# Halving the last two products of a down projection, and of a pair of value pieces, in front of runs of 256-column matmuls

## The chip, the cores and the metric

The kernel runs on one core of a Trainium2 chip. The metric is the device time of one execution in microseconds, as the median of several runs. Profiles are of one execution; a profile's span goes from its first to its last instruction, which is a little less than the time of the execution.

## The reference

A decoder trunk of two layers on 256 tokens of width 1024, in float32. The first layer mixes tokens by dilated sliding-window attention, the second by forgetting attention; each is followed by a SwiGLU feed-forward part.

```python
D_MODEL = 1024; SEQ = 256; DEPTH = 2; N_HEADS = 16; HEAD_DIM = 64
D_FF = 2816

def swiglu(h, w_gu, w_down):
    gu = h @ w_gu
    g, u = gu[..., :D_FF], gu[..., D_FF:]
    return (jax.nn.silu(g) * u) @ w_down

def reference(x, ...):
    h = x
    for i in range(DEPTH):
        j = i // N_MIXERS
        if i % N_MIXERS == 0:
            h = h + dilated_mixer(rmsnorm(h, a_norm[j]), a_w_in[j], a_w_out[j])
        else:
            h = h + forgetting_mixer(rmsnorm(h, b_norm[j]), b_w_in[j], b_f[j], b_w_out[j])
        h = h + swiglu(rmsnorm(h, ffn_norm[i]), ffn_w_gu[i], ffn_w_down[i])
    return rmsnorm(h, final_norm)
```

The dilated mixer projects to queries, keys and values of three groups (window and dilation 128/1, 512/4, 2048/16), the forgetting mixer to one set of queries, keys and values and a gate; both end in an output projection `w_out`.

## The kernel before

**Products in three parts.** Every large matrix product is taken in float32r, with each operand split into a high and a low part: ScalarE writes the high part (line 73), VectorE the rest (line 74). `mm3` then issues three matmuls into the same PSUM tile: high by high (line 172), high by low (173), low by high (174). Its `stat` operand is the stationary one, of 128 columns, for which TensorE loads weights before each matmul; `mov` is the moving one, of 256 or 512 columns. Each matmul instruction has a weight load of its own, also where two in a row use the same stationary block.

**Weights.** `weights` hands out the weights piece by piece (128 x 2048) in the order of the list `order`, and starts the loads of two pieces ahead. `piece` loads a piece in two halves over SyncE's queue, each of which is then split by ScalarE and VectorE. `wh` and `wl` have four buffers, `raw` five.

**Projections.** `proj_feat` computes 128 output features for all 256 tokens: stationary are the weights, moving is `xt` (the normed input, features on partitions), so these are runs of 256-column products, 8 x 3 = 24 for each call, 48 for a piece with two calls. `proj_tok` has 128 tokens stationary and 256 weight columns moving. `proj_pair` computes two value pieces together, with the 512 columns of a half piece moving; it is called once for each half of the contraction (`half` 0, then 1), for both halves of the tokens (`t`), four `k` each, so 24 products of 512 columns.

**First layer.** The list `a_units` sets the order: for each of four quads of heads the queries and keys of three groups (`proj_feat`), and value pieces by `proj_pair` or `proj_tok`. Score, transpose and value matmuls of a quad (`scores_a`, `trans_a`, `pv_a`) are put behind later units by `later`. The scores of group 0 also go through `mm3`, 12 products of 256 columns for each pair of heads (tiles `kr` and `qz` in the profile).

**Feed-forward part (`ffn`).** There are 22 pieces of gate and up weights (`gu`) and 11 of down weights (`dn`). `up_with` computes the gate and up columns of a piece by two calls of `proj_feat` (tiles `ps_mm` and `ps_tr`), and the gated product from them (lines 671, 673). `down(j, t)` adds the part of down weights `j` to the accumulators of token half `t`: two blocks of 512 output columns (tiles `ps_sc` for `t` 0 and `ps_o` for `t` 1), two halves `f` of the contraction each, so 4 x 3 = 12 products. The loop is

```python
for f in range(2, NF):
    if f > 2:
        up(f)
    if f % 2 == 0:
        j = f // 2 - 1
        dn[j] = weights(f"dn{l}", j)
        down(j, 0)
        if j < LATE:
            down(j, 1)
```

with `NF` 22 and `LATE` 8. In the steady part two `up` (96 products of 256 columns) alternate with two `down` (24 of 512). From `j` = 8 on, the second token half's `down` is put off to the end. The last `up` (piece 21) has a higher priority, by which the scheduler puts it ahead of `down(9, 0)`, so that three `up` (144 products) follow `down(8, 0)`. In the last `down` of the second layer (`own`) the upper 512 columns go in two blocks of 256.

The order on each engine is that of the program, apart from such priorities, and is fixed before the run; engines wait for one another by semaphores.

Of the kernel before, what the change touches and what calls it, by code (L numbers as in the profile page):

```python
# [19 lines left out]
KT = D // P  # L20
# [11 lines left out]
def trunk(ctx: ExitStack, tc: tile.TileContext, T, out):  # L32
    nc = tc.nc
# [6 lines left out]
    ALL = slice(None)  # L40

    def first():

        return tc.high_priority(offset=300)

    def psum(tag):
        return ps.tile([P, 512], F32, tag=tag, name=f"ps_{tag}", bufs=2)
# [65 lines left out]
    NJ = NF // 2  # L113
    LATE = NJ - 3
# [13 lines left out]
    def weights(nm, i):  # L128
        upto = order.index((nm, i)) + AHEAD
        while state["next"] <= min(upto, len(order) - 1):  # L130
            key = order[state["next"]]
            ready[key] = piece(key)
            state["next"] += 1
        return ready.pop((nm, i))
# [32 lines left out]
            split(xt, lambda x: x[:, half * 4:half * 4 + 4, t * P:(t + 1) * P],  # L167
                  tr.rearrange("p (k c) -> p k c", k=4))

    def mm3(o, stat, mov, start, stop):  # L170
        (sh, sl), (mh, ml) = stat, mov
        nc.tensor.matmul(o, sh, mh, start=start, stop=False)  # L172
        nc.tensor.matmul(o, sh, ml, start=False, stop=False)  # L173
        return nc.tensor.matmul(o, sl, mh, start=False, stop=stop)  # L174

    def both(pair, *idx):
        return tuple(x[idx] for x in pair)


    def early(x, b):  # L180

        x = x.rearrange("p (n b) -> p b n", b=2)
        return x if b is None else x[:, b]
# [17 lines left out]
    def proj_pair(xt, w, os, half, ts=range(2), by_time=False):  # L201

        for t in ts:
            for k in range(half * 4, half * 4 + 4):
                i = k % 4 * 512
                st = both(xt, ALL, k, ALL)
                last = mm3(os[t], [early(x, t) if by_time else x[:, t * P:(t + 1) * P] for x in st],
                           both(w, ALL, slice(i, i + 512)), k == 0, k == KT - 1)
        return last

    def proj_feat(xt, w, o, c, hook=None):

        last = None
        for k in range(KT):
            between(k, hook, last)
            last = mm3(o, both(w, ALL, slice(k * 256 + c * P, k * 256 + (c + 1) * P)),
                       both(xt, ALL, k, ALL), k == 0, k == KT - 1)
        return last


    def p_tile(n=512, dtype=F32, name="p"):
        return ap.tile([P, 768], dtype, tag="p", name=name, bufs=6)[:, :n]
# [60 lines left out]
    o = psum("o")  # L283
# [10 lines left out]
    for i, c in enumerate(room):  # L294
        b = 1 + (i > 1)
        n = S + 512
# [35 lines left out]
    def square(i):  # L332
        return nc.scalar.activation(part[i].rearrange("p (j s) -> p j s", s=S), xs[i], AF.Square, scale=D ** -0.5)
# [5 lines left out]
    for k in range(KT):  # L339
        if k % 4 == 0:  # L340
            w = tuple(wp.tile([P, 2048], F32R, tag=y, name=y, bufs=4) for y in ("wh", "wl"))
        g, u = g_a[:, k:k + 1], slice(k % 4 * 512, k % 4 * 512 + 512)
        with first(), in_order(cut):
            if k == 0:
                a = nc.vector.tensor_scalar(hi[:, k], xk[k], g, None, op0=ALU.mult)
            else:
                a = nc.scalar.activation(hi[:, k], xk[k], AF.Copy, scale=g)
            b = nc.vector.scalar_tensor_tensor(lo[:, k], xk[k], g, hi[:, k].bitcast(F32), op0=ALU.mult,
                                               op1=ALU.subtract)
            with in_order((a, b)):  # L350
                cut = split(w, lambda y: y[:, u], wk[k])
        if k in (1, 5, 7):
            with first(), in_order(cut):
                a = [square(i) for i in {1: (0, 1), 5: (2,), 7: (3,)}[k]][-1]
                cut = (a, plus(part[0], part[1]) if k == 1 else cut[1])
        for y, z in ((0, 0), (1, 0), (0, 1)):
            for t in range(2):
                nc.tensor.matmul(lead[t], xt[y][:, k, t * P:(t + 1) * P], w[z][:, u], start=k + y + z == 0,
                                 stop=k == KT - 1 and z == 1)
# [7 lines left out]
    with first(), in_order(cut):  # L367
        a = square(4)
# [124 lines left out]
    for i, (hq, g, w) in enumerate(a_units):  # L493
        quad = quads[hq]
        if i == 3:
            o = o_next
        elif i:
            wt = weights("a_in", hq * 9 + g * 3 + w)
        if i != 3 and (w < 2 or g == 0 and hq > 1):
            o = psum("mm")  # L500
# [7 lines left out]
        if i in (24, 31):  # L508
            x.append(hrow("x"))
            t = len(x) - 1  # L510
            nc.sync.dma_start(x[t], T["x"][t * P:(t + 1) * P, :])
        if w < 2:
# [35 lines left out]
            elif g == 0:  # L548

                y = ap.tile([P, 2, 2, S], F32R, tag="h", name="kr", bufs=4)  # L550
                f, q = q, (y[:, 0], y[:, 1])
                split(q, lambda y: y.rearrange("p a (b n) -> p a b n", b=2), f.rearrange("p a (n b) -> p a b n", b=2))
            quad["fm"][g, w] = q
            if w == 1:

                j = i + (hq == 0)
# [5 lines left out]
                if g == 2:  # L562
                    later(j + 1, softmax_a, quad)
                    j = 9 * hq + 11 + 2 * (hq == 0)
# [80 lines left out]
    def ffn(l, hs, xt, grow, mid):  # L645
        acc = {}
        acts = {}

        def act(f):
            if f % 2 == 0:  # L650
                acts[f // 2] = tuple(p_tile(512, F32R, f"a{y}") for y in "hl")
            return acts[f // 2], lambda y: y[:, (f % 2) * S:(f % 2 + 1) * S]

        def gated(g, u, shape):
            sa = ap.tile([P, 512], F32, tag="qr", name="sa", bufs=3)
            sg, a = (sa[:, i * S:(i + 1) * S].rearrange("p (a b) -> p a b", a=shape) for i in range(2))
            nc.scalar.activation(sg, g, AF.Silu)
            nc.vector.tensor_tensor(a, u, sg, op=ALU.mult)
            return a

        def up(f):
            wt = weights(f"gu{l}", f)
            with first() if f == NF - 1 else nullcontext():
                up_with(f, wt)

        def up_with(f, wt):
            sa = ap.tile([P, 512], F32, tag="qr", name="sa", bufs=3)
            sg, a = (sa[:, i * S:(i + 1) * S] for i in range(2))
            g, u = (psum(tag)[:, :S] for tag in ("mm", "tr"))
            proj_feat(xt, wt, g, 0)  # L670
            nc.scalar.activation(sg, g, AF.Silu)  # L671
            proj_feat(xt, wt, u, 1)
            nc.vector.tensor_tensor(a, u, sg, op=ALU.mult)  # L673
            split(*act(f), a)

        def down(j, t, by_f=None):

            wt = dn[j]
            if j == 0:
                acc[t] = [psum(("sc", "o")[t]) for _ in range(2)]  # L680
            cols = [(0, 512, acc[t][0][:, :512]), (512, 512, acc[t][1][:, :512])]
            own = l == 1 and t == 1 and j == NJ - 1
            if own:

                acc[t][1:] = psum("mm"), psum("tr")
                cols[1:] = (512, 256, acc[t][1][:, :256]), (768, 256, acc[t][2][:, :256])
            nf = [(c, f) for c in cols for f in range(2)]
            if by_f is not None:
                nf = [(c, f) for f in by_f for c in cols]
            for (a, b, o), f in nf:  # L690
                i = mm3(o, both(acts[j], ALL, slice(f * S + t * P, f * S + (t + 1) * P)),
                        both(wt, ALL, slice(f * D + a, f * D + a + b)), f == 0 and (j == 0 or own and a >= 512),
                        f == 1 and (j == NJ - 1 or l * t * a > 0 and j == NJ - 2))
            return i


        dn = {}
        head = []
        for f in range(3):
            head.append((weights(f"gu{l}", f), psum((("o", "o", "mm"), ("mm", "mm", "o"))[l][f])))  # L700
            proj_tok(xt, head[f][0], head[f][1][:, :S], 0,
                     hook=(2, lambda: norm_t(*hs[1], grow, xt, 1)) if f == 2 else None)
        for f in range(3):
            o = head[f][1]
            proj_tok(xt, head[f][0], o[:, S:], 1)
            ov = o.rearrange("p (a c b) -> p a c b", a=2, c=2)
            a = gated(ov[:, :, 0, :], ov[:, :, 1, :], 2)
            tr = psum("tr")
            for t in range(2):
                nc.tensor.transpose(tr[:, t * P:(t + 1) * P], a[:, t, :], ident)  # L710
            split(*act(f), tr[:, :S])
# [3 lines that stand above are left out]
            if f % 2 == 0:  # L715
                j = f // 2 - 1
                dn[j] = weights(f"dn{l}", j)
                down(j, 0)
                if j < LATE:
                    down(j, 1)  # L720
        dn[NJ - 1] = weights(f"dn{l}", NJ - 1)
        down(LATE, 1)
        last = down(NJ - 1, 0, (0, 1))
        res = [residual(acc[0], hs[0][0], f"hf{l}0")]
        with tc.issue_after(last.ins):
            down(NJ - 2, 1)
            if l == 0:
                down(NJ - 1, 1, (0,))
            else:
                h1 = hs[1][0][:, 512:]  # L730
                with first():
                    nc.vector.tensor_tensor(h1, acc[1][1], h1, op=ALU.add)
            mid(res[0])
            down(NJ - 1, 1, (1,) if l == 0 else None)
        res.append(residual(acc[1], hs[1][0], f"hf{l}1") if l == 0 else (acc[1], hs[1][0]))
        return res
# [9 lines left out]
    def mid(h0):  # L746
        nxt["g"] = load_grow(2)
        nxt["xt"] = xt_tile()
        norm_t(*h0, nxt["g"], nxt["xt"], 0)

    hs = ffn(0, hs, xt, g_f, mid)
    xt, g_b = nxt["xt"], nxt["g"]

# [121 lines left out]
    for i in range(2):  # L875
        last = proj_pair(xt, ws[i], os, i, (1,))
# [6 lines left out]
    for i, (hq, w) in enumerate(b_units):  # L883
# [3 lines left out]
        o = psum("mm")  # L887
        if w < 2:
# [15 lines left out]
            if w == 1:  # L904
                j = i + 1
# [35 lines left out]
    for o, (a, b) in zip(acc, ((0, 512), (512, 256), (768, 256))):  # L941
        s = slice(a, a + b)
# [108 lines left out]
```

## Time and profile before

| | |
|---|---|
| median of 3 runs | 771.75 us (771.35 to 771.86) |
| the profiled execution | 771.89 us |
| its span | 770.0 us |
| TensorE busy | 759.2 us (99%), 5760 matmuls |
| weight loads busy | 703.2 us (91%), 5760 |
| VectorE, ScalarE busy | 509.9 us (66%), 401.0 us (52%) |
| DMA | 135.01 MB, 175 GB/s in the mean |
| TensorE clock granted | 0.999 |

In the timeline a row gives the start and the length of an instruction in microseconds, its engine, its line, and the tiles it writes and reads (output, then sources). Matmuls overlap: the next one starts before the record of the last one ends, so the distance between two starts tells what a matmul costs, and its recorded length does not. A row ending in x1 is a single instruction. In a row of the view by stretches stand the stretch, its length, and for TensorE, weight loads, VectorE, ScalarE and GpSimd the busy time and the number of instructions, then the clock, the share of the DMA engines and GB/s. A row of waits says which engine waited for which, the total, how often and the longest.

### The profile page before, as it was taken

What the parts mean: (1) busy time and instruction counts of PE and PEld (TensorE: products, weight loads), DVE (VectorE), ACT (ScalarE), POOL (GpSimd) and SP (SyncE); (2) the same over time, 40 slices, a digit from 0 to 9 for tenths busy, and PEclk for the clock granted to TensorE, in tenths of its full rate; (3) what the DMA queues carried; (4) which work ended last, traced back from release to release, by engine and by line L of the source; (5) the groups of instructions that cost most, each with busy time, mean ns of one, the idle gap of its engine ahead of it and who ended that gap; (6) DMA issues with size and microseconds to landing.
All of it is one profiled execution on the core that took longest, in us unless ns stands there. A gap on an engine that the chain in (4) does not pass through costs nothing.

```text
span 770.0 us, 14046 instructions
## 1 busy us (share of the span) xinstructions
PE 759.2 (99%) x5760; PEld 703.2 (91%) x5760; DVE 509.9 (66%) x758; ACT 401.0 (52%) x664; POOL 33.8 (4%) x51
## 2 busy tenths in 40 slices
PE   9999999999999999999999999999999999999996
PEld 7998999999998799999999988999889999999995
DVE  6998987976978476545456374887756645456533
ACT  7745639448538455434454354586655444344421
POOL 1110000010010000000000003100000000000000
PEclk9999999999999999999999999999999999999999
DMA  8865461743663267565566444644326665656601
GB/s 319 288 206 170 162 217 57 242 168 98 202 213 120 95 222 240 181 194 189 186 202 231 147 156 145 218 139 128 115 92 220 216 206 175 198 186 206 204 2 54
DMA packets 38352, 135.01 MB, mean 175 GB/s; under 512 B 4368, under 2 KB 5648, under 8 KB 38288
## 3 DMA queue, kind: packets, MB, share of 16 engines
q1 hardware_dynamic: 38144, 134.01, 52.4%
q8 instruction: 45, 0.74, 0.4%
q14 instruction: 19, 0.16, 0.1%
q10 hardware_dynamic: 144, 0.10, 0.0%
HBM read 133.05 MB, written 1.05 MB: 174 GB/s over the span
## 4 chain that ended last, share of the span: by engine, by line
PE 86%; DVE 5%; ACT 3%; issue 2%; DMA 2%; POOL 1%; SPq 0%; POOLq 0%; DVEq 0%; ACTq 0%
PE ps_mm L172 15%; PE ps_mm L174 15%; PE ps_mm L173 15%; PE ps_tr L172 5%; PE ps_tr L174 5%; PE ps_tr L173 5%; PE ps_sc L174 4%; PE ps_sc L172 4%; PE ps_sc L173 4%; PE ps_o L174 3%; PE ps_o L173 3%; PE ps_o L172 3%; PE ps_tr L265 2%; PE ps_o L276 2%; DVE wl L74 2%
## 5 line engine op out<-in xcount | busy, mean ns | idle before, releaser
L73 ACT ACTIVATE wh<-raw 128x1024 fp32r<-128x1024 f32 x236 | 243.2, 1055 | 224.4 <-PE ps_tr L173 70.5
L74 DVE TENSOR_TENSOR wl<-raw,wh 128x1024 fp32r<-128x1024 f32 x236 | 284.2, 1220 | 104.7 <-ACT wh L73 104.5
L172 PE MATMUL ps_mm<-xt,wh 128*128 128x256 f32 x816 | 229.2, 281 | 0.0
L174 PE MATMUL ps_mm<-xt,wl 128*128 128x256 f32 x816 | 227.7, 279 | 0.1
L173 PE MATMUL ps_mm<-xt,wh 128*128 128x256 f32 x816 | 227.5, 279 | 0.0
L174 PEld LDWEIGHTS ps_mm<-xt,wl 128*128 128x128 f32 x816 | 154.8, 190 | 0.5 <-DVE wl L74 0.5
L173 PEld LDWEIGHTS ps_mm<-xt,wh 128*128 128x128 f32 x816 | 153.5, 188 | 0.9
L172 PEld LDWEIGHTS ps_mm<-xt,wh 128*128 128x128 f32 x816 | 153.2, 188 | 1.1
L173 PE MATMUL ps_tr<-xt,wh 128*128 128x256 f32 x304 | 85.3, 281 | 0.0
L174 PE MATMUL ps_tr<-xt,wl 128*128 128x256 f32 x304 | 85.3, 281 | 0.0
L172 PE MATMUL ps_tr<-xt,wh 128*128 128x256 f32 x304 | 85.1, 281 | 0.0
L673 DVE TENSOR_TENSOR sa<-ps_tr,sa 128x256 f32<-128x256 f32 x38 | 16.1, 425 | 81.6 <-PE ps_tr L174 81.4
L172 PE MATMUL ps_mm<-wh,xt 128*128 128x256 f32 (+1 forms) x176 | 59.6, 339 | 1.6 <-DVE fm L402 1.6
L173 PE MATMUL ps_mm<-wl,xt 128*128 128x256 f32 (+1 forms) x176 | 58.5, 332 | 0.0
L174 PE MATMUL ps_mm<-wh,xt 128*128 128x256 f32 (+1 forms) x176 | 58.4, 332 | 0.0
L174 PEld LDWEIGHTS ps_tr<-xt,wl 128*128 128x128 f32 x304 | 58.3, 192 | 0.0
L173 PEld LDWEIGHTS ps_tr<-xt,wh 128*128 128x128 f32 x304 | 57.1, 188 | 0.0
L172 PEld LDWEIGHTS ps_tr<-xt,wh 128*128 128x128 f32 x304 | 56.9, 188 | 0.0
L172 PEld LDWEIGHTS ps_mm<-wh,xt 128*128 128x128 f32 x176 | 33.5, 190 | 5.5 <-issue 2.0
L174 PEld LDWEIGHTS ps_mm<-wh,xt 128*128 128x128 f32 x176 | 33.5, 190 | 3.6 <-DVE xt L74 0.3
L173 PEld LDWEIGHTS ps_mm<-wl,xt 128*128 128x128 f32 x176 | 33.5, 190 | 2.9
L671 ACT ACTIVATE sa<-ps_mm 128x256 f32<-128x256 f32 x38 | 14.3, 381 | 33.5 <-PE ps_mm L174 33.5
(237 smaller groups left out, 1154.2 us busy)
## 6 DMA issues: line engine op xcount, KB each, us to landing
raw<-in_gu SPq DMA_DIRECT2D x88, 512.0 KB, 4.7
raw<-in_a_in SPq DMA_DIRECT2D x68, 512.0 KB, 4.5
raw<-in_dn SPq DMA_DIRECT2D x44, 512.0 KB, 4.7
raw<-in_b_in SPq DMA_DIRECT2D x24, 512.0 KB, 5.0
raw<-in_a_out SPq DMA_DIRECT2D x8, 512.0 KB, 4.5
raw<-in_b_out SPq DMA_DIRECT2D x8, 512.0 KB, 4.2
grow<-in_norms SPq DMA_DIRECT2D x4, 512.0 KB, 5.9
x<-in_x SPq DMA_DIRECT2D x2, 512.0 KB, 5.6
```

The lines of the kernel that those rows point to most:

```text
L73: return (nc.scalar.activation(view(hi), src, AF.Copy), nc.vector.tensor_tensor(view(lo), src, view(hi).bitcast(F32), op=ALU.subtract))
L74: nc.vector.tensor_tensor(view(lo), src, view(hi).bitcast(F32), op=ALU.subtract))
L172: nc.tensor.matmul(o, sh, mh, start=start, stop=False)
L173: nc.tensor.matmul(o, sh, ml, start=False, stop=False)
L174: return nc.tensor.matmul(o, sl, mh, start=False, stop=stop)
L265: nc.tensor.transpose(tr[:, i * P:(i + 1) * P], b, ident)
L276: nc.tensor.matmul(o[h * HD:(h + 1) * HD], v[:, c:c + HD], w(h), start=start, stop=stop)
L671: nc.scalar.activation(sg, g, AF.Silu)
L673: nc.vector.tensor_tensor(a, u, sg, op=ALU.mult)
```

## The change

`mm3` gets an argument `narrow`. Where it is set, the second and the third product are issued as two matmuls each, over the first and the second half of the moving columns, with the same stationary operand; the first product stays whole. It is set

- in `down`, for the last product triple of the call (upper 512 columns, second half of the contraction), where the call asks for it: the second token half's call for weights 0 to 7, and the first token half's call for weights 8 and 9;
- in `proj_pair`, for the last triple of a pair (last `k`, second token half).

Sums and their order within each output element stay as they were.

```diff
-    def mm3(o, stat, mov, start, stop):
+    def mm3(o, stat, mov, start, stop, narrow=False):
+
         (sh, sl), (mh, ml) = stat, mov
         nc.tensor.matmul(o, sh, mh, start=start, stop=False)
-        nc.tensor.matmul(o, sh, ml, start=False, stop=False)
-        return nc.tensor.matmul(o, sl, mh, start=False, stop=stop)
+        n = o.shape[-1]
+        for s, m, end in ((sh, ml, False), (sl, mh, stop)):
+            for c in range(0, n, n // 2 if narrow else n):
+                u = slice(c, c + (n // 2 if narrow else n))
+                last = nc.tensor.matmul(o[:, u], s, m[:, u], start=False, stop=end and u.stop == n)
+        return last
...
     def proj_pair(xt, w, os, half, ts=range(2), by_time=False):
...
-                           both(w, ALL, slice(i, i + 512)), k == 0, k == KT - 1)
+                           both(w, ALL, slice(i, i + 512)), k == 0, k == KT - 1, k == KT - 1 and t == 1)
...
-        def down(j, t, by_f=None):
+        def down(j, t, by_f=None, narrow=False):
...
-                        f == 1 and (j == NJ - 1 or l * t * a > 0 and j == NJ - 2))
+                        f == 1 and (j == NJ - 1 or l * t * a > 0 and j == NJ - 2), narrow and (a, b, f) == (512, 512, 1))
...
-                down(j, 0)
+                down(j, 0, narrow=j >= LATE)
                 if j < LATE:
-                    down(j, 1)
+                    down(j, 1, narrow=True)
```

## The prediction

> **What bounds the kernel now.** The page comes first: busy time, and the chain that ended last.
>
> ```profile
> span 770.0 us, 14046 instructions
> ...
> PE 759.2 (99%) x5760; PEld 703.2 (91%) x5760; DVE 509.9 (66%) x758; ACT 401.0 (52%) x664; POOL 33.8 (4%) x51
> ...
> PE 86%; DVE 5%; ACT 3%; issue 2%; DMA 2%; POOL 1%; SPq 0%; POOLq 0%; DVEq 0%; ACTq 0%
> ```
>
> TensorE is busy 99% of the span and holds 86% of the chain, so the time falls only if the matmuls themselves come closer together. A busy share can't show that, because consecutive matmuls overlap in the records. What counts is the distance between starts. I read it next from the timeline of TensorE, in one feed-forward iteration of layer 0: 24 products of 512 columns (`down`), then 96 of 256 columns (two `up`, 48 each).
>
> ```profile
> 307.25 0.39 PE L172 MATMUL ps_sc<-wh,ah 128*128 128x512 f32 x1
> ...
> 312.47 0.39 PE L174 MATMUL ps_o<-wh,al 128*128 128x512 f32 x1
> 312.69 0.28 PE L172 MATMUL ps_mm<-xt,wh 128*128 128x256 f32 x1
> 312.81 0.28 PE L173 MATMUL ps_mm<-xt,wh 128*128 128x256 f32 x1
> ...
> 324.00 0.39 PE L172 MATMUL ps_sc<-wh,ah 128*128 128x512 f32 x1
> ```
>
> The 512-column products stand (312.69 - 307.25) / 24 = 226.7 ns apart, the 256-column ones (324.00 - 312.69) / 96 = 117.8 ns. That is more than half of 226.7. The same `proj_feat` products run closer together elsewhere: between these two rows of the first layer lie 191 of them (four units of 48, less the first).
>
> ```profile
> 69.60 0.28 PE L173 MATMUL ps_mm<-xt,wh 128*128 128x256 f32 x1
> ...
> 91.25 0.27 PE L265 MATMUL ps_tr<-ident,p 128*128 128x128 f32 x1
> ```
>
> (91.25 - 69.60) / 191 = 113.35 ns, exactly half of 226.7. So one shape, with the same kinds of operands, has two paces, 113.35 and 117.8 ns, and each is held over whole runs: 191 products at the one, 96 at the other. The difference is 4.45 ns a product. All 18 `up` runs that directly follow 512-column products in the two feed-forward parts (eight of 96 and one of 144 in each layer) are of the slow kind. So is this run of 144 in the first layer, which follows the value pair of the third quad:
>
> ```profile
> 182.55 0.28 PE L172 MATMUL ps_mm<-xt,wh 128*128 128x256 f32 x1
> ...
> 199.51 0.27 PE L265 MATMUL ps_tr<-ident,p 128*128 128x128 f32 x1
> ```
>
> (199.51 - 182.55) / 144 = 117.8 ns. The question is therefore what sets a run's pace, and the entries tell. When `proj_feat` follows other 256-column products without a gap, it settles at the fast pace. Here it follows the scores of group 0, which themselves go at 120 ns:
>
> ```profile
> 100.77 0.28 PE L174 MATMUL ps_sc<-kr,qzl 128*128 128x256 f32 x1
> 100.89 0.29 PE L172 MATMUL ps_mm<-xt,wh 128*128 128x256 f32 x1
> 101.01 0.28 PE L173 MATMUL ps_mm<-xt,wh 128*128 128x256 f32 x1
> 101.14 0.28 PE L174 MATMUL ps_mm<-xt,wl 128*128 128x256 f32 x1
> 101.25 0.28 PE L172 MATMUL ps_mm<-xt,wh 128*128 128x256 f32 x1
> 101.36 0.28 PE L173 MATMUL ps_mm<-xt,wh 128*128 128x256 f32 x1
> ...
> 102.16 0.28 PE L174 MATMUL ps_mm<-xt,wl 128*128 128x256 f32 x1
> ```
>
> The first four take 101.36 - 100.89 = 0.47 us, 117.5 ns each; the next seven take 0.80 us, 114 ns each. The seven entries of this kind (near 48, 94, 101, 148, 157, 208 and 217 us) all end fast, and so does the one behind a `proj_tok` run that stood at 118 ns, which drops to 0.11 us between starts at once:
>
> ```profile
> 478.89 0.28 PE L172 MATMUL ps_mm<-xt,wh 128*128 128x256 f32 x1
> ...
> 479.35 0.28 PE L173 MATMUL ps_mm<-xt,wh 128*128 128x256 f32 x1
> 479.46 0.28 PE L174 MATMUL ps_mm<-xt,wl 128*128 128x256 f32 x1
> ```
>
> Eight of eight entries from 256 columns are fast, none of nineteen from 512 columns is. The nearest to an exception: one entry from 512 columns starts on the second product of `mm3` (the first had been issued earlier) and is fast at once, 0.11 us between its first starts; but it belongs to `proj_tok`.
>
> ```profile
> 464.27 0.39 PE L174 MATMUL ps_mm<-wh,xt 128*128 128x512 f32 x1
> 464.51 0.28 PE L173 MATMUL ps_sc<-wl,xt 128*128 128x256 f32 x1
> 464.62 0.28 PE L174 MATMUL ps_sc<-wh,xt 128*128 128x256 f32 x1
> ```
>
> **The change part by part.** *Halved products.* At 25 places the second and third product of one `mm3` become two of 256 columns each: ten `down` calls per layer (the second row half of weights 0 to 7, the first row half of 8 and 9) and five value pairs (four in the first layer, one in the second). That adds 50 matmuls and 50 weight loads, with no DMA, no wait, and nothing on another engine. The price comes from rows of the last `down`, where 256-column products with the same operands stand behind 512-column ones:
>
> ```profile
> 761.21 0.28 PE L172 MATMUL ps_mm<-wh,ah 128*128 128x256 f32 x1
> 761.32 0.28 PE L173 MATMUL ps_mm<-wl,ah 128*128 128x256 f32 x1
> 761.44 0.28 PE L174 MATMUL ps_mm<-wh,al 128*128 128x256 f32 x1
> 761.56 0.28 PE L172 MATMUL ps_mm<-wh,ah 128*128 128x256 f32 x1
> 761.68 0.28 PE L173 MATMUL ps_mm<-wl,ah 128*128 128x256 f32 x1
> ```
>
> Four starts take 0.47 us, 117.5 ns each, so two halves are 235 ns against 226.7: +8.3 ns, and 50 of them +0.42 us, all on the path. The ends are 113.35 ns a half (nothing) and 120 ns, the scores' pace (13.3 x 50 = +0.67 us). A gain is excluded, as no run of 256 columns stands closer than 113.35. I take +0.42, since these rows have the operands of `down`.
>
> *Pace of the runs behind them.* No row of before has 512 columns, four halves and then `proj_feat`. The ends are no effect and the fast pace from the first product; a loss is bounded by the 120 ns of the scores (the rivals). I take the entry at 100.89, the nearest in kind: four products without gain, then 4.45 ns each. A run of 96 gains 92 x 4.45 = 0.41 us, a run of 144 gains 140 x 4.45 = 0.62. Runs that directly follow a halved product: eight of 96 and one of 144 in each feed-forward part (16 x 0.41 + 2 x 0.62 = 7.8 us), and the 144 at 182.55 (0.62). Sum 8.4 us.
>
> *Places without a run behind.* The pairs of the first two quads are followed by small score or value matmuls, the fourth quad's by 512 columns of the output projection, the second layer's by two transposes of the gates, and `down` of weights 9 by further 512-column products, because `up` of the last piece has priority and goes ahead of it. That is six places that only pay; their price is in the 0.42. The 48 products behind the transposes at 199.51 could also turn fast, up to 48 x 4.45 = 0.21 us; I count nothing.
>
> *What must keep up.* In the slow run the other engines have room:
>
> ```profile
> 312.70:323.90 11.20, 11.20 (x97) 11.20 (x96) 5.49 (x6) 5.10 (x7) 0.00 (x0) 1.00 0.60 189
> DVE sa L673 <- PE ps_tr L174: 81.4, 35, 4.9
> ```
>
> VectorE is busy 5.49 of 11.2 us, ScalarE 5.10, the DMA engines 0.60, and VectorE waits 81.4 us in all for `up` to end. A run that is 0.4 us shorter is covered by that slack. If it were not, the saving would come back as TensorE waiting for a piece of weights, at most the same 0.4 us a run.
>
> **Sum.** -8.4 + 0.42 = -8.0 us. The profiled run took 771.89 us, of which the span is 770.0, 0.14 us above the median of the runs. So the span should be 762.0 us, and the median 771.75 - 8.0 = 763.8 us. With free halves and all products fast (16 x 96 + 3 x 144 + 48 = 2016) it is 2016 x 4.45 = 9.0 less, 762.8.
>
> A rule of the Trainium skill speaks against all this: TensorE: Matmul & The Clock Gate, section Back-to-back issue gap, gives the isolated gap between matmuls by width alone, 262 cycles at 256 columns and 518 at 512 on the full clock. By it, an estimate, each halved product costs 2 x 262 - 518 = 6 cycles (2.5 ns), 50 of them 0.1 us, and what stands ahead of a run changes nothing: 771.9 us. The trace does not agree, with 113.35 and 117.8 ns for one width. The section also says that in a stream the load and the matmul set the distance together, which leaves room for two paces.
>
> **The rivals.** *The entry stays slow* (0.15). The pace may hang on something other than width, such as the longer column of earlier 256s: the seven score entries had twelve or more ahead, here there are four. Then only the halves count: 772.2 us (771.8 to 772.4). Against it: in the rows at 761.21 three products suffice to change the distance from 0.11 to 0.12 us.
>
> *A part turns* (0.10). Some entries turn and others don't, or a run falls back where its weights change. Half the gain gives 771.75 - 4.2 + 0.42 = 768.0, anything from 764.6 to 770. Against it: the 191 products at 113.35 ns cross three changes of weights, and the entries of the feed-forward part are all alike.
>
> *The runs take the pace of the halves* (0.07), the slower side. The scores hold 120 ns; if `proj_feat` kept it, each product would lose 2.2 ns: 1968 (those 2016 without the 48 behind the transposes) x 2.2 + 0.67 = 5.0 us, 776.8. It is slower by 0.2% once some 400 products stay at 120. Against it: at 100.89 just that pace went ahead, and it was gone after four products.
>
> **How the numbers follow.** The forecast has 0.68, the rivals 0.15, 0.10 and 0.07. The likeliest case's own range is 762.6 to 764.6. With the partial case it holds 0.78, so the range must reach to the case without effect: 762.6 to 772.4. A measurement of this kernel tells about 0.2% (1.5 us) from no change. Faster by more: 0.68 + 0.10 = 0.78; within: 0.15; slower: 0.07.
>
> **What would show it.** In the timeline after: four halves some 113 to 120 ns apart, then about four `proj_feat` starts at 116 to 122, then 113.3; feed-forward runs of 96 at 10.9 us for 11.3. If the first start distances behind the halves are 118 and stay so, the step on the entry is wrong. If TensorE shows waits for weights in these parts, the step on cover is.

## The result, and the profile after

| | before | after |
|---|---|---|
| median | 771.81 us (771.35 to 774.0) | 765.17 us (764.49 to 766.52) |
| the profiled execution | 771.89 us | 765.6 us |
| its span | 770.0 us | 763.8 us |

The ratio is 0.9911 (95% interval 0.9887 to 0.9934): 6.6 us faster, where 8.0 us was forecast. The page of after, in the lines that answer to those shown of before:

```profile
span 763.8 us, 14146 instructions
...
PE 752.6 (99%) x5810; PEld 698.7 (91%) x5810; DVE 509.8 (67%) x758; ACT 401.0 (53%) x664; POOL 33.6 (4%) x51
...
PE 88%; DVE 4%; ACT 3%; issue 2%; DMA 2%; SPq 0%; POOL 0%; POOLq 0%; DVEq 0%; ACTq 0%
```

TensorE issues 50 matmuls more and is busy 6.6 us less. It still holds the chain. The timeline of TensorE, at the same feed-forward entry as before (a row with x2 joins two matmuls of one line; its start is that of the first):

```profile
312.62 0.39 PE L173 MATMUL ps_o<-wh,ah 128*128 128x512 f32 x1
312.85 0.40 PE L178 MATMUL ps_o<-wl,ah 128*128 128x256 f32 x2
313.08 0.40 PE L178 MATMUL ps_o<-wh,al 128*128 128x256 f32 x2
313.32 0.29 PE L173 MATMUL ps_mm<-xt,wh 128*128 128x256 f32 x1
313.44 0.28 PE L178 MATMUL ps_mm<-xt,wh 128*128 128x256 f32 x1
313.56 0.28 PE L178 MATMUL ps_mm<-xt,wl 128*128 128x256 f32 x1
313.68 0.28 PE L173 MATMUL ps_mm<-xt,wh 128*128 128x256 f32 x1
313.79 0.28 PE L178 MATMUL ps_mm<-xt,wh 128*128 128x256 f32 x1
...
324.22 0.39 PE L173 MATMUL ps_sc<-wh,ah 128*128 128x512 f32 x1
```

The 96 products take 324.22 - 313.32 = 10.90 us, before 11.31. The records hold starts to the nanosecond, so the distances can be read finer than the rows round them: the four halves stand 114, 119 and 120 ns apart, the run starts 120 ns behind the last, and goes on with 121, 121, 116, 114, 114 and then 113 to 114 to its end. All 18 feed-forward runs look like this, and so does the run behind the third quad's value pair:

```profile
183.89 0.40 PE L178 MATMUL ps_mm<-wl,xt 128*128 128x256 f32 x2
184.13 0.40 PE L178 MATMUL ps_mm<-wh,xt 128*128 128x256 f32 x2
184.37 0.28 PE L173 MATMUL ps_mm<-xt,wh 128*128 128x256 f32 x1
...
200.70 0.27 PE L270 MATMUL ps_tr<-ident,p 128*128 128x128 f32 x1
```

(200.70 - 184.37) / 144 = 113.4 ns, before 117.8. VectorE still has room in the faster run, and it waits less for `up` (before 81.4 us):

```profile
313.30:324.20 10.90, 10.90 (x98) 10.90 (x97) 5.48 (x6) 5.10 (x7) 0.00 (x0) 1.00 0.57 188
DVE sa L678 <- PE ps_tr L178: 74.5, 34, 4.6
```

Where the span went can be read from the starts of a few landmarks in the timelines of TensorE: the first 512-column pair, the first `proj_feat` behind the first quad's small scores (69.38 us before), the first `down` (290.16), the gate matmul of the second layer (471.04), its first `down` (594.97) and the end of the last matmul (762.80). In us between them, for every kernel in this document:

| kernel | to the pair | to 69.4 | to 290.2 | first feed-forward part | second mixer | second feed-forward part |
|---|---|---|---|---|---|---|
| before | 54.81 | 14.57 | 220.79 | 180.88 | 123.93 | 167.83 |
| after | 54.61 | 16.56 | 219.94 | 177.40 | 123.68 | 164.31 |
| e1_down_only | 54.59 | 14.16 | 220.78 | 177.36 | 123.71 | 164.32 |
| e2_last_product | 54.25 | 14.55 | 220.75 | 177.22 | 123.52 | 164.17 |
| e3_whole_last | 54.09 | 14.76 | 219.86 | 177.55 | 123.95 | 164.44 |
| e4_turned_start | 55.91 | 14.50 | 220.72 | 180.90 | 124.21 | 167.85 |
| e5_placed | 53.57 | 14.74 | 219.80 | 177.23 | 124.06 | 164.18 |
| e6_far_halves | 54.54 | 16.52 | 219.92 | 181.02 | 123.81 | 167.97 |
| e7_inside | 54.05 | 16.31 | 219.93 | 179.48 | 124.08 | 166.43 |
| e8_after_again | 54.06 | 16.52 | 220.75 | 177.39 | 124.08 | 164.33 |
| e9_third_quad | 54.08 | 16.54 | 219.86 | 177.43 | 123.79 | 164.32 |
| e10_pairs_only | 54.77 | 14.40 | 220.77 | 180.88 | 124.27 | 167.84 |
| e11_first_only | 54.28 | 16.34 | 220.72 | 177.38 | 123.79 | 164.36 |
| e12_second_only | 54.28 | 14.92 | 220.77 | 177.40 | 123.72 | 164.31 |

The parts that the forecast is about give -0.85, -3.48 and -3.52, together -7.85 us. The second column takes 2.0 us back: 0.43 us of it is a longer wait, the rest goes with the half clock behind it. There TensorE waits once for VectorE; before, then after:

```profile
59.36 0.48 PE L172 MATMUL ps_mm<-wh,xt 128*128 128x512 f32 x1 [1.58 <-DVE fm L402]
```

```profile
59.59 0.75 PE L173 MATMUL ps_mm<-wh,xt 128*128 128x512 f32 x1 [2.01 <-DVE fm L407]
60.13 0.63 PE L178 MATMUL ps_mm<-wl,xt 128*128 128x512 f32 x1
...
58.00:60.00 2.00, 0.41 (x1) 0.45 (x2) 2.00 (x6) 0.00 (x0) 0.00 (x0) 0.90 0.83 254
60.00:62.00 2.00, 2.00 (x6) 1.52 (x6) 2.00 (x4) 0.00 (x0) 0.00 (x0) 0.50 0.61 217
```

The last two rows are stretches; the third number from the end is the granted clock. It is 0.50 just behind the wait (1.00 before), and 512-column products stand 0.43 us apart there for 0.23. Whether that comes with the change is taken up in e8 to e10.

### The profile page after: what moved, and what is told of

Read it like the earlier page. It is cut to its first block, busy times and chain, and to the rows that moved or that the text cites. A ratio compares the mean times of both kernels' runs of the same rounds, so it can differ in the third digit from the quotient of the medians.

```text
span 763.8 us, 14146 instructions
## 1 busy us (share of the span) xinstructions
PE 752.6 (99%) x5810; PEld 698.7 (91%) x5810; DVE 509.8 (67%) x758; ACT 401.0 (53%) x664; POOL 33.6 (4%) x51
## 4 chain that ended last, share of the span: by engine, by line
PE 88%; DVE 4%; ACT 3%; issue 2%; DMA 2%; SPq 0%; POOL 0%; POOLq 0%; DVEq 0%; ACTq 0%
PE ps_mm L178 30%; PE ps_mm L173 16%; PE ps_tr L178 9%; PE ps_sc L178 8%; PE ps_o L178 6%; PE ps_tr L173 5%; PE ps_sc L173 4%; PE ps_o L173 3%; PE ps_tr L270 2%; PE ps_o L281 2%; DVE wl L74 1%; PE ps_sc L837 1%; ACT wh L73 1%; DMA otl<-in_lead 1%; DMA raw<-in_a_in 1%
## 5 line engine op out<-in xcount | busy, mean ns | idle before, releaser
L178 PE MATMUL ps_tr<-xt,wh 128*128 128x256 f32 x304 | 83.8, 276 | 0.0
L173 PE MATMUL ps_tr<-xt,wh 128*128 128x256 f32 x304 | 83.6, 276 | 0.0
L178 PE MATMUL ps_sc<-wh,al 128*128 128x512 f32 (+1 forms) x82 | 31.4, 387 | 0.0
```

The lines of the kernel that those rows point to most:

```text
L178: last = nc.tensor.matmul(o[:, u], s, m[:, u], start=False, stop=end and u.stop == n)
```

## The experiments

Each diff is against the changed kernel, unless it says otherwise.

**e1_down_only: halves in down alone.** In `proj_pair`:

```diff
...
-  k == 0, k == KT - 1, k == KT - 1 and t == 1)
+  k == 0, k == KT - 1)
```

> The halves in the down calls stay, those in the five value pairs are taken out. Theory (a run of 256-column products takes its pace at its entry, and halves directly in front of it make the entry fast): all 18 feed-forward runs keep 113.4 ns a product, only the run of 144 behind the third quad's value pair falls back to 117.8 ns, and the 48 products after its transposes with it. That is 0.8 us back, less five places at 0.02 us: 0.7 us more than the changed kernel, some 5.9 to 7.7 us less than before. Rival (the gain is some general effect of the changed program, not of each place): the third quad's run stays at 113.4 ns.

764.37 us against 772.85, ratio 0.9895 (0.9879 to 0.9912). The 18 runs are fast, and the third quad's run is slow again:

```profile
181.92 0.28 PE L173 MATMUL ps_mm<-xt,wh 128*128 128x256 f32 x1
...
198.88 0.27 PE L270 MATMUL ps_tr<-ident,p 128*128 128x128 f32 x1
```

(198.88 - 181.92) / 144 = 117.8 ns. The stage that holds it takes 220.78 us, as before (220.79), where the changed kernel has 219.94. So the halves in front of a run turn that run, and the 0.85 us belongs to the pair.

**e2_last_product: only the third product in halves** (in `down` and in the pairs).

```diff
         for s, m, end in ((sh, ml, False), (sl, mh, stop)):
-            for c in range(0, n, n // 2 if narrow else n):
-                u = slice(c, c + (n // 2 if narrow else n))
+            half = narrow and s is sl
+            for c in range(0, n, n // 2 if half else n):
+                u = slice(c, c + (n // 2 if half else n))
```

> Only the third product of each chosen triple is halved, the second stays whole. Theory (it is the 256-column product directly ahead that counts): the runs are fast all the same, 96 products in 10.9 us, and each place costs one halved product less, some 5 to 13 ns, 0.1 to 0.3 us in all less than the changed kernel. Rival (it takes several 256-column products, until they stand 120 ns apart, to turn the entry): with two halves the runs stay at 117.8 ns, 11.3 us for 96, and the time is that of before, 771.8 to 772.4.

764.02 us against 772.85, ratio 0.9891 (0.9876 to 0.9906). Two halves are enough for the 18 runs (stages 177.22 and 164.17). They were not enough for the third quad:

```profile
181.75 0.39 PE L179 MATMUL ps_mm<-wh,xt 128*128 128x256 f32 x2
181.98 0.28 PE L173 MATMUL ps_mm<-xt,wh 128*128 128x256 f32 x1
182.10 0.28 PE L179 MATMUL ps_mm<-xt,wh 128*128 128x256 f32 x1
...
198.94 0.27 PE L271 MATMUL ps_tr<-ident,p 128*128 128x128 f32 x1
```

(198.94 - 181.98) / 144 = 117.8 ns, directly behind 256-column products. Here the run starts 113 ns behind the second half; in the feed-forward part it starts 118 to 120 ns behind it. That 256 columns stand ahead is not sufficient.

**e3_whole_last: the first and second product in halves, the third whole**, so that 512 columns stand directly ahead of the run.

```diff
-        nc.tensor.matmul(o, sh, mh, start=start, stop=False)
-        for s, m, end in ((sh, ml, False), (sl, mh, stop)):
-            for c in range(0, n, n // 2 if narrow else n):
+        for s, m, go, end in ((sh, mh, start, False), (sh, ml, False, False), (sl, mh, False, stop)):
+            half = narrow and s is sh
+            for c in range(0, n, n // 2 if half else n):
...
```

> The first and the second product of each chosen triple are halved, and the third stays whole, so that four halves stand at the same places, but a 512-column product lies between them and the run. Theory (what stands directly ahead counts): the runs are slow again, 117.8 ns, 11.3 us for 96, and only the price of the halves is left: 772 to 772.6 us. Rival (the additional weight loads, or halves anywhere near, set the pace): the runs stay fast, 764 to 766 us.

764.29 us against 772.85, ratio 0.9892 (0.9877 to 0.9907). The theory of the prediction, that the width directly ahead sets the pace, falls here:

```profile
310.73 0.40 PE L178 MATMUL ps_o<-wh,al 128*128 128x512 f32 x1
310.96 0.40 PE L178 MATMUL ps_mm<-xt,wh 128*128 128x256 f32 x2
...
321.86 0.39 PE L178 MATMUL ps_sc<-wh,ah 128*128 128x512 f32 x1
```

(321.86 - 310.96) / 96 = 113.5 ns. All 18 runs and the third quad's turn, some two products later than in the changed kernel, with a whole 512-column product ahead. That product took 233 ns to the run's first start, where it takes 226.7 in a stream.

**e4_turned_start: no halves; each `up` begins with high by low.** Against the kernel before:

```diff
+        if turned:
+            nc.tensor.matmul(o, sh, ml, start=start, stop=False)
+            nc.tensor.matmul(o, sl, mh, start=False, stop=False)
+            return nc.tensor.matmul(o, sh, mh, start=False, stop=stop)
...
```

> No product is halved; instead the first triple of each up run takes its three products in another order, high by low first, then low by high, then high by high. Theory: the entry is from 512 columns as before, the runs stay at 117.8 ns, and the time is that of before, 771.5 to 772.1 us. Rival (it is the product with which a run begins, as in the one fast entry from 512 columns at 464.51 us of before): the runs go at 113.4 ns, 763.5 us, without any halves to pay for.

771.91 us against 772.85, ratio 0.9998 (0.9987 to 1.0009). All 18 runs stay slow (180.90 and 167.85 us), so the operands of the first product do not decide. The exception named in the prediction (a `proj_tok` run that starts on the second product) fits the table below instead: it starts 231 ns behind the 512-column product ahead of it, 4 ns later than in a stream.

**e5_placed: halves only ahead of a run.** The third product alone in `down`, none at weights 9, both products in the third quad's pair alone, and both in the last triple of each output projection, ahead of 54 `proj_tok` products.

```diff
...
-                down(j, 0, narrow=j >= LATE)
+                down(j, 0, narrow=(2,) if j == LATE else ())
-                    down(j, 1, narrow=True)
+                    down(j, 1, narrow=(2,))
...
-            proj_pair(xt, wt, lead, half, by_time=g == 0)
+            proj_pair(xt, wt, lead, half, by_time=g == 0, narrow=(1, 2) if hq == 2 else ())
...
-                    part(t, acc, cols(range(6, KT)))
+                    part(t, acc, cols(range(6, KT)), (1, 2))
```

> Halves only where a run of 256-column products follows: in down the third product alone (second token half of weights 0 to 7, first token half of weights 8; none at weights 9), in the value pairs the second and third product of the third quad's alone, and, new, the second and third product of the last triple of each output projection, ahead of the 54 proj_tok products of the next feed-forward part (118 ns apart before, and after). Theory (halves shift the phase in which a run is entered; a start distance of 121 ns or more among the first products, then 113.3): the 18 feed-forward runs fast as with the third product alone (stages 177.2 and 164.2 us), the third quad fast (219.9), and the two runs of 54 turn with a chance of one half, 54 x 4.45 = 0.24 us each. Against the kernel before -7.3 - 0.85 and 0 to -0.5: -8.2 to -8.7 us, ratio 0.989. Rival (the third quad's turn in the changed kernel was chance, not the halves): 0.85 less gained, stage 220.8.

762.78 us (762.69 to 763.07) against 772.19, ratio 0.9884 (0.9871 to 0.9897); on the same chip the changed kernel (e8) took 765.78. Part of the distance to e8 is the clock (below); all four executions of e5 are also under the changed kernel's fastest, 763.54. Both runs of 54 turned; the second one:

```profile
570.76 0.40 PE L178 MATMUL ps_sc<-wh,otl 128*128 128x256 f32 x2
571.00 0.28 PE L173 MATMUL ps_mm<-wh,xt 128*128 128x256 f32 x1
571.11 0.28 PE L178 MATMUL ps_mm<-wl,xt 128*128 128x256 f32 x1
```

The products behind it stand 113 ns apart, in every other kernel here 118. So `proj_tok`, with the tokens stationary, has the two paces too.

**e6_far_halves: the halves one triple earlier**, three whole products between them and the run.

```diff
...
-  narrow and (a, b, f) == (512, 512, 1))
+  narrow and (a, b, f) == (512, 512, 0))
```

> In down the halves stand in the triple before the last (upper 512 columns, first half of the contraction) instead of the last, so that three whole 512-column products (0.68 us) lie between them and the run; value pairs as in the changed kernel. Theory (a phase that is carried from product to product, also through 512 columns): the 18 runs turn fast, some products later, feed-forward stages 177.4 and 164.3 us, in all as the changed kernel, -8.0 us against before. Rival (three 512-column products wash the phase out; what counts is the last product or two): the runs stay at 117.8 ns, stages 181.0 and 168.0, only the third quad's 0.85 us is left, less 0.3 to 0.6 for halves without effect: -0.3 to -0.6 us.

771.70 us against 772.19, ratio 0.9996 (0.9982 to 1.001). Neither expectation holds whole: the 16 runs of 96 stay slow, both runs of 144 turn. The entries of one of each kind:

```profile
313.42 0.39 PE L178 MATMUL ps_o<-wh,al 128*128 128x512 f32 x1
313.65 0.28 PE L173 MATMUL ps_mm<-xt,wh 128*128 128x256 f32 x1
...
428.47 0.40 PE L178 MATMUL ps_sc<-oth,al 128*128 128x512 f32 x1
428.71 0.28 PE L173 MATMUL ps_mm<-xt,wh 128*128 128x256 f32 x1
```

The slow one starts 228 ns behind the last 512-column product, the fast one 236.

**e7_inside: no halves in `down`; inside the run instead** the second and third product of its first triple (odd `up`) as two matmuls of 128 columns each.

```diff
...
-            proj_feat(xt, wt, g, 0)
+            proj_feat(xt, wt, g, 0, narrow=f % 2 == 1)
...
```

> No halves in down. Instead the second and third product of the first triple of every odd up (3, 5 ... 21), that is inside each run of 96 and 144 just behind its entry, are issued as two matmuls of 128 columns each; value pairs as in the changed kernel. Theory (any matmul of another length shifts the phase, wherever it stands): the products behind go at 113.3 ns, 18 runs give -7.0 us, and the 128-column matmuls cost between nothing and 0.09 us a product, if a matmul of 128 columns takes as long as one of 256 (20 x 2 x 0.12 = 4.6 us at the most): -0.85 - 7.0 + 0 to 4.6 = -7.9 to -3.3 us against before. Rival (it must be a 256-column product ahead of the run's first): the runs stay at 117.8 ns, -0.85 + 0 to 4.6 us.

768.90 us against 772.19, ratio 0.9962 (0.9947 to 0.9976). All 18 runs turn, but each part gains 1.40 us instead of 3.5:

```profile
312.67 0.28 PE L173 MATMUL ps_mm<-xt,wh 128*128 128x256 f32 x1
312.79 0.34 PE L178 MATMUL ps_mm<-xt,wh 128*128 128x128 f32 x2
312.96 0.39 PE L178 MATMUL ps_mm<-xt,wl 128*128 128x128 f32 x2
313.19 0.33 PE L173 MATMUL ps_mm<-xt,wh 128*128 128x256 f32 x1
313.36 0.28 PE L178 MATMUL ps_mm<-xt,wh 128*128 128x256 f32 x1
...
323.81 0.39 PE L173 MATMUL ps_sc<-wh,ah 128*128 128x512 f32 x1
```

From 312.79 to 313.36 stand five matmuls in 0.57 us; three products need 0.34 at the fast pace. The starts behind the four of 128 columns stand 61, 112, 113 and 112 ns apart, and 167 ns follow behind the 256-column product after them. Taken together, a matmul of 128 columns costs about 113 ns here, as long as one of 256, and the run gains 11.31 - 11.14 = 0.17 us.

**The entry distance.** With these runs one number separates the fast from the slow: the distance from the start of the last product ahead of a run to the run's first start. Over the profiles of before, after and all twelve kernels of this section, for `proj_feat` runs of 20 products or more that directly follow a product of `mm3`, without a stall:

| last product ahead | its start to the run's first | fast runs | slow runs |
|---|---|---|---|
| 256 columns | 113 to 115 ns | 0 | 6 |
| 256 columns | 116 to 121 ns | 222 | 0 |
| 512 columns | 226 to 229 ns | 0 | 75 |
| 512 columns | 233 to 236 ns | 57 | 0 |

(Two kinds are left out: the first run of the start-up, which stops several times, and the 18 runs of e7, entered at 226 or 227 ns and turned only by the matmuls of 128 columns inside them.) Against the fast paces of 113.35 and 226.7 ns, a run that starts up to 2.3 ns late is slow and one that starts 2.7 ns late or more is fast. No experiment sets this distance itself. Halves were placed and the distance was read, so it is a mark that sorts the runs; what makes a run late is only partly seen, as the halves of e6 made two runs late and left sixteen on time. The rule was read off the kernels e1 to e10 and the two profiles; the next two kernels were run to test it.

**e11_first_only and e12_second_only: one product of `down` in halves**, the first with two whole products behind it, or the second with one. For e11 (for e12 it is `i == 1`); the pairs are whole in both:

```diff
+        for i, (s, m, go, end) in enumerate(((sh, mh, start, False), (sh, ml, False, False), (sl, mh, False, stop))):
+            half = n // 2 if narrow and i == 0 else n
+            for c in range(0, n, half):
+                u = slice(c, c + half)
...
```

> In down only the first product of the last triple is halved, the second and third are whole, so two whole 512-column products stand between the halves and the run; value pairs whole. This puts a rule to the test that was read off the profiles so far: what decides is the start distance right ahead of the run (from the last product before it to the run's first). From a 256-column product, 113 to 115 ns gave a slow run (6 of 6) and 116 to 121 a fast one (206 of 206); from a 512-column product, 226 to 229 a slow one (73 of 73) and 233 to 236 a fast one (21 of 21). So each of the 18 feed-forward runs must go by its own entry distance: 229 or less slow, 233 or more fast. All fast: stages 177.3 and 164.2 us, -7.0 us against before; all slow: 181.1 and 168.0, +0.2. Rival (what counts is the number of halves shortly ahead, four or two directly ahead; the distance is only a trace of that): the runs go alike whatever their distance, slow here.

> In down only the second product of the last triple is halved, one whole 512-column product (the third) stands between the halves and the run; value pairs whole. The same rule of the entry distance: a run entered at 229 ns or less goes at 117.8 ns, one entered at 233 or more at 113.3. All fast: stages 177.3 and 164.2 us, -7.0 us against before; all slow: 181.1 and 168.0, +0.2. Rival (the number of halves counts): two halves with a whole product behind them leave the runs slow whatever the distance.

765.22 us (ratio 0.9914, 0.9897 to 0.993) and 764.67 us (0.9911, 0.9896 to 0.9926), against 771.78. All 36 feed-forward entries lie at 233 to 236 ns and all 36 runs are fast; the third quad's run in both is entered at 227 ns and slow. An entry of e11:

```profile
313.32 0.40 PE L178 MATMUL ps_o<-wh,al 128*128 128x512 f32 x1
313.56 0.40 PE L178 MATMUL ps_mm<-xt,wh 128*128 128x256 f32 x2
...
324.45 0.39 PE L178 MATMUL ps_sc<-wh,ah 128*128 128x512 f32 x1
```

(324.45 - 313.56) / 96 = 113.4 ns. The rival, that two halves with whole products behind them are too few, falls: one halved product does it. All 18 entries of each kernel fell on the late side, so the runs don't show late and early entries behind the same halves; the whole pairs give the two early ones.

**e8_after_again, e9_third_quad, e10_pairs_only: the clock near 60 us.** e8 is the changed kernel; e9 has halves in the third quad's pair alone and `down` as changed; e10 has all pairs as changed and `down` whole.

> The changed kernel once more, beside the others on one chip. Theory (its one stall near 60 us, with the clock at half for some 3 us, was of that execution and not of the change): no granted clock under 0.9 between 58 and 64 us, span 2.2 us shorter than the first profile's, 761.6 us, -8.4 us against before. The run of 118 proj_tok products near 476 us may be entered fast or slow (0.4 us). Rival (the stall comes with the change): the clock falls again at that place, span 763.8.

> The changed kernel, but of the value pairs only the third quad's has halves; the pairs of the first, second and fourth quad and of the second layer, which have no run behind them, are whole. Down as changed. Theory (the stall near 60 us and the half clock after it belong to single executions of any of these kernels, since no changed matmul stands ahead of it): 4 x 0.02 us saved, so the time of the changed kernel's executions at a mean clock of 0.997 or more, 764.3 us, and executions at 0.995 some 2 us longer as often as before, -7.5 to -8.5 us against before at like clock. Rival (the halved pairs of the first quads bring the stall): no execution under 0.997, no granted clock under 0.9 at 58 to 64 us.

> Only the value pairs have halves (all five, second and third product, as changed), down is whole. Theory: the run of 144 behind the third quad's pair and the 48 behind the transposes after it go at 113.3 ns, -0.85 us in the stage of 220.8 us, 5 x 0.02 us for the halves; the 18 feed-forward runs stay at 117.8 ns: -0.8 us at like clock, 0.1%, not to be told from no change by the times but by the stage. Rival (the halved pairs of the first quads bring the stall near 60 us): executions at 0.995 in most, +1.4 us against before.

765.78 us (ratio 0.9914, 0.9898 to 0.993), 764.93 (0.991, 0.9894 to 0.9925) and 772.0 (0.9999, 0.9989 to 1.0009). The stretch from 60 to 62 us of e9, then of e10:

```profile
60.00:62.00 2.00, 2.00 (x6) 1.52 (x6) 2.00 (x4) 0.00 (x0) 0.00 (x0) 0.50 0.55 215
```

```profile
60.00:62.00 2.00, 2.00 (x10) 1.48 (x8) 2.00 (x4) 0.00 (x0) 0.00 (x0) 1.00 0.59 225
```

e8's clock fell too (0.59 in this stretch), against the theory of a single execution. The rival, that the halved pairs of the first quads bring it, falls with e9: it has whole pairs there, no changed matmul stands ahead of that wait, and it loses the clock. e10, with halved ones, kept it in its profile, which decides nothing by itself.

The traces show when the clock falls. They list the stretches of granted clock, and up to the last fall these are whole multiples of 3.41 us in all 14 profiles; the loss near 60 us is one such slice at half. What goes before it is the idle time of TensorE inside the slice ahead. The two slices concerned, in e7 (a wait of 1.77 us), then in e12 (1.94 us, but cut in two by the end of a slice):

```profile
56.26:59.67 3.41, 1.64 (x8) 1.09 (x7) 3.41 (x7) 0.46 (x1) 0.14 (x1) 1.00 0.75 256
59.67:63.09 3.42, 3.42 (x10) 2.44 (x8) 3.42 (x5) 0.00 (x0) 0.00 (x0) 0.50 0.56 174
```

```profile
55.58:58.99 3.41, 1.66 (x8) 1.04 (x6) 3.41 (x6) 1.08 (x2) 1.00 (x2) 1.00 0.75 244
58.99:62.40 3.41, 3.23 (x27) 2.51 (x31) 3.41 (x6) 0.14 (x1) 0.00 (x0) 1.00 0.60 217
```

TensorE is idle for 1.77 us of the first slice in e7, and for less than 1.76 us in e12. Over all slices of the 14 profiles, 1.77 us of idle or more was always followed by half the clock (near 60 us in six profiles, and behind the last matmul in each), and less than 1.76 us never. In e8 the fall came 1.3 us after the wait had ended, with the end of the slice. So the loss hangs on how long VectorE keeps TensorE waiting (1.18 to 2.02 us) and on where the slices lie. What sets either is not shown.

In the profiles the loss goes with a mean clock of 0.995 for the execution (after, e6, e7, e8, e9, e11), and 0.997 or more goes without it. By that mark the kernel before has such executions too: of its 54 timed beside these kernels, 40 are at 0.997 or more (median 771.62 us) and 14 below (773.11). Six of the 13 beside e1 to e4 are among these, which is why its median is 772.85 there. Of the changed kernel's ten, four are at 0.997 or more (764.27) and six below (766.16); of e9's six it is four below, of e10's twelve six, of e5's four none. Whether the change makes the loss more frequent stays open. At like clock the change is worth 764.27 - 771.62 = -7.35 us.

e10's stage of 220.77 us seems to deny the third quad's gain. It doesn't: that run is fast in e10, and in exchange a run of 192 products near 69 us, entered behind small score matmuls, is slow there, as in e8 and in no other kernel. The profile of after, of the same kernel as e8, has that run fast: behind a wait and small matmuls the pace can differ from one execution to the next.

## Why the prediction was right

**Price of the halves.** Predicted 8.3 ns a product, 17 a place. The four halves take from 312.85 to 313.32, 0.47 us for 0.453: some 20 ns a place. Right.

**Entry and pace.** Predicted four products without gain, then 113.3 ns; runs of 96 at 10.9 us. Measured 121, 121, 116, 114, and 10.90 us. All 19 runs turned. Right in size, but the reason, the width ahead, was wrong. "Eight of eight entries from 256 columns are fast" was true of that trace, and yet the width was not what sorted those entries. Seven came from the scores, at 120 ns, and one at 116, all late by the table above. The entries from 512 columns came at 226 or 227 ns, on time. e2's third quad (256 columns ahead, 113 ns, slow) and e3 (512 columns ahead, 233 ns, fast) part the two readings. The rows showed 0.12 us ahead of the fast entries; the step went from there to the width instead of to the distance. That it held for all 19 runs was in part luck: their halves stood 117 to 120 ns ahead, on the late side, where the same width at 113 ns in e2 turned nothing.

**The run that was taken as safe.** By the width rule the 96 products behind a `proj_tok` run in the second layer stay fast. Here they went slow:

```profile
476.24 0.28 PE L178 MATMUL ps_sc<-wh,xt 128*128 128x256 f32 x1
476.36 0.28 PE L173 MATMUL ps_mm<-xt,wh 128*128 128x256 f32 x1
476.47 0.28 PE L178 MATMUL ps_mm<-xt,wh 128*128 128x256 f32 x1
476.59 0.28 PE L178 MATMUL ps_mm<-xt,wl 128*128 128x256 f32 x1
476.71 0.28 PE L173 MATMUL ps_mm<-xt,wh 128*128 128x256 f32 x1
```

They were entered at 115 ns, before at 116. That costs up to 96 x 4.45 = 0.43 us, though the second mixer as a whole was not longer (123.68 for 123.93).

**Terms of the sum.** The 48 products behind the third quad's transposes, counted as nothing with up to 0.21 us open, turned too; with them the 0.62 us became 0.85. The feed-forward parts gave 3.48 and 3.52, forecast 8 x 0.41 + 0.62 less 0.17 = 3.73 each. In all -7.85 us for -8.0.

**Cover.** Right: no wait for weights in these parts, and VectorE waits 6.9 us less for `up` while 7 us of matmul time went.

**The median.** Forecast 763.8, measured 765.17. The term that is missing is the wait near 60 us with the half clock behind it, 2.0 us in the profiled execution. No step looked at it, because before had the wait (1.58 us) without the loss. At like clock some 0.5 us to the forecast remain (764.27 for 763.8), about the size of the run that was taken as safe.

**The rivals.** By the rule that the isolated gap goes by width alone (the Trainium skill, TensorE: Matmul & The Clock Gate, Back-to-back issue gap) nothing would have been gained; 3.5 us in each feed-forward part speak against it. The halves did turn the runs, all of them, and none took the halves' 120 ns beyond its third product.

## What to carry to other kernels

Where TensorE is the bound at 99% busy, compare the distance between starts for one shape in different places: a few per cent between two runs of the same instruction is a gain that no busy share shows. On this chip a run of 256-column float32r products settled within its first few on one of two paces and kept it to its end, unless matmuls of another width stood inside it (e7). One product halved ahead of it, with at most two whole ones between, was worth 0.4 us per 96 products wherever it made the run start 3 ns or more late, and nothing where it did not (the third quad of e2). So read the entry in the timeline of the changed kernel, put halves only where such a run follows, and prefer 256-column halves to 128-column ones. Test the reading by a case in which the two candidate causes part, before a rule is made of a perfect count.

## What the runs showed of the hardware

Two paces for one instruction, 113.35 and 117.8 ns, each held over as many as 192 products, across changes of weights and of the PSUM tile; which of them a run takes behind products of `mm3` goes with 3 ns in how late it is entered (2.3 ns late was slow, 2.7 fast, as far as records in whole nanoseconds tell). Why the later start is the better one is not shown by these records.

A 128-column matmul of this kind costs about 113 ns in e7, no less than a 256-column one at 113.35.

The clock is granted in slices of 3.41 us. It fell to half for one slice behind waits of 1.77 to 2.02 us in six profiles, and did not behind waits of 1.18 to 1.94 us in the other eight: the length of the wait alone does not decide, but the idle time within one slice does (1.77 us and more, against less than 1.76). The Trainium skill (TensorE: Matmul & The Clock Gate, What's actually happening) has a free-running window of 3413 ns behind the clock's fall. The slices of 3.41 us in the traces agree with that. That page's table of goals (Why this matters for your kernels) warns only of idle gaps over about 3 us, and here 1.77 us inside one slice was enough.
